# A two-layer hybrid block in one planned instruction stream: a low-rank rest product moved from 64 to 128 rows, and RWKV row sums as single fp32 products

## The chip, the core and the metric

The kernel runs on one core of a Trainium2 chip. The metric is device time in microseconds (us) of one execution. Before the change three executions took 1990.63, 1990.66 and 1992.5 us; the median is 1990.66 us. The engines are TensorE (PE, with its weight loads listed apart as PEld), VectorE (DVE), ScalarE (ACT), GpSimd (POOL) and SyncE (SP, which issues almost all transfers).

## The reference, cut to what matters

Two layers work on a sequence of 1024 tokens and 1024 channels. Each layer normalises its input with an adaptive scale and shift, projects it onto 4680 columns, runs three branches on parts of the result (chunked latent attention, a chunked state-space scan, and an RWKV-7 recurrence), and adds the gated output projection back. The change touches the RWKV branch:

```python
w_lo = token_shift(w_lo, mu_w)
a_lo = token_shift(a_lo, mu_a)
w = jnp.exp(-DECAY_SCALE * jax.nn.sigmoid((w0 + jnp.tanh(w_lo) @ w_lora_b).astype(f32)))
a = jax.nn.sigmoid((a0 + a_lo @ a_lora_b).astype(f32))
kk = k * heads(k_k)
kk = kk / jnp.maximum(jnp.sqrt(jnp.sum(kk * kk, axis=-1, keepdims=True)), 1e-12)
y = wkv7_scan(r, w, k, v, -kk, kk * a)
y = y + jnp.sum(r * k * r_k.astype(f32), axis=-1, keepdims=True) * v
```

There are 8 heads of 64 channels. `w_lo` and `a_lo` have 64 channels each, so the two low-rank products contract over 64 values. The two sums over a head's 64 channels (of the squared key, and of `r * k * r_k`) are the row sums of this document.

## The kernel before, in words

Channels lie on the 128 partitions and tokens on the free axis. The sequence is cut into two halves of 512 tokens, so that with two layers there are four stages. A stage first does its dense work: 8 tiles of normalised input, each split into a high part in fp32r and the rest (`a`, `b` in `make_h`, 16 tiles of the pool `h2`), and 37 column tiles of the input projection. Each column tile takes 24 products of 128x128 weights with 512 tokens: high weight with high input, high with rest, rest with high, for 8 contraction tiles. In the trace these are the rows `ps<-h,wh` and `ps<-h,wl`, since the tiles of `h2` are called `h`. ACT copies a finished tile out of PSUM (`ct<-ps`), and a transfer puts it into memory (`U<-ct`). For stages 2 and 3 the dense work begins with the output projection of layer 0, whose inputs are split into pairs of `h2` tiles by `y_split`.

The branches read `U` back. RWKV works on a pair of heads at a time, four pairs in a stage, so the function `rwkv_a1` and its follower `rwkv_a2` run 16 times. For each pair:

- two low-rank products. A product in fp32r keeps only part of the mantissa, so the input is split. `wa[0]` holds the high part of the 64 decay channels twice, once for each half of the partitions; the weight tile `lora` holds the high part of the 64 weight rows in one half of the partitions and their rest in the other. The first product over 128 rows therefore adds high x high and high x rest. A second product over 64 rows adds the input's rest (`wa[2]`) times the high weights. The same is done for the other 64 channels. These rows read `ps<-wa,lora`; the 64-row ones are `64*128 64x512`.
- the row sum `pq` (line 788 of the kernel before): the squared key is split by ACT into `leafh` and by DVE into `leafl`, and two fp32r products with two columns of a block-of-ones matrix (`bones_r`) give 2 rows of 512 sums.
- the row sum `pbn` (line 834): the same with all 128 columns of `bones_r`, which spreads each head's sum over its 64 partitions.

The row sum `pq` is copied to SBUF, goes through memory and scales a triangular inverse (`tinv_a`, the long chain of small DVE operations on `Q`, `rq` and `tmp`). `pbn` is multiplied by `v` and stored as `sp` for the end of the branch.

Beside this runs preparation for the next stage: loads of the modulation matrix land in `ct` tiles and DVE adds them up into `ac` (`ada_acc`); when a sum is complete, PE transposes it (`ps<-cst,ac`, in `colsum`) and DVE writes 4 columns of scale or shift (`md`).

Nothing is issued as it is written. Every operation is recorded, and a planner (`Plan.order`) then lists all of them in the order of a modelled time: each has a cost from a table, a rank, dependencies, and waits for a free buffer of its pool. RWKV has a higher rank than the other branches, and both have a higher rank than the `ac` sums. Each engine then executes its own list strictly in order. The planner's table charges extra for a product whose contraction needs another row mode than the one before it (`DRAIN`), and charges an fp32 product with at most 64 weight columns one short price whatever its length. These are the planner's assumptions, not measurements. A change of one operation therefore moves all lists. All recorded operations have one line in the trace (L396), so the rows are told apart by their tiles.

Of the kernel before, what the change touches and what calls it, by code (L numbers as in the profile page):

```python
# [10 lines left out]
F32R = mybir.dt.float32r  # L11
I32 = mybir.dt.int32
AF = mybir.ActivationFunctionType
# [4 lines left out]
P = 128  # L18
KT = 8
HT = 512  # L20
# [23 lines left out]
C_ID, C_MD, C_SM, C_BO, C_IF, C_SG, C_S4, C_M1 = 0, 128, 256, 768, 896, 897, 898, 902  # L44
NCST = 1030

N_H2, N_RT, N_RI, N_RQ, N_RL, N_CT, N_WR, N_WL, N_WH, N_B2 = 18, 5, 2, 2, 3, 4, 3, 3, 3, 17
N_BK, N_GG, N_BX, N_AR, N_BM, N_TT, N_RV, N_GT = 1, 2, 3, 1, 1, 2, 2, 2
RW_T = 0
N_EZ = 1  # L50
# [21 lines left out]
SG0 = "bbgggggg"  # L72
SBP, SBC, SCH = "ra", "ra", 2
SRB = "tf"
PQ = 1
PB = 1
PX = "b2"
WAT = "rv"
LOT = "rl"
# [318 lines left out]
def hybrid_layers_kernel(ctx: ExitStack, tc: tile.TileContext, A, out):  # L398
    nc = tc.nc
    plan = Plan(tc)  # L400
    V, S, G, PE, SP = (plan.engine(e, q) for e, q in ((nc.vector, "V"), (nc.scalar, "S"), (nc.gpsimd, "G"),
                                                      (nc.tensor, "P"), (nc.sync, "Q")))
    TQ, AL, AS, BL, BM, BS, EQ = SP, S, S, S, SP, S, SP

    cpool = ctx.enter_context(tc.tile_pool(name="cpool", bufs=1))
    lpool = ctx.enter_context(tc.tile_pool(name="lpool", bufs=1))
# [16 lines left out]
    def nm(s):  # L423
        ctr[0] += 1
        return f"{s}{ctr[0]}"
# [26 lines left out]
    def s1(n, tag=None, bufs=None):  # L452
        if bufs:
            return sm.tile([P, n], F32, name=nm("s"), tag=tag or f"s{n}", bufs=bufs)
        return sm.tile([P, n], F32, name=nm("s"), tag=tag or f"s{n}")

    def bank(tag):
        return ps.tile([P, HT], F32, name=nm("ps"), tag=tag, bufs=PSB[tag])

    def mm(o, lhsT, rhs, start=True, stop=True):  # L460
        PE.matmul(o, lhsT, rhs, start=start, stop=stop)

    def f32(ap):
        return ap.bitcast(F32)
# [7 lines left out]
    def hs_(e):  # L472
        return slice(64 * e, 64 * e + 64)
# [7 lines left out]
    bones = cst[:, C_BO:C_BO + 128]  # L481
# [3 lines left out]
    Ez = [cpool.tile([P, 2, 4, 128], F32, name=f"Ez{i}") for i in range(N_EZ)]  # L485
    for z in Tz + Ez:
        G.memset(z, 0.0)
    turn = [0]
    nhalf = cpool.tile([P, 8], F32, name="nhalf")
    V.memset(nhalf, -0.5)  # L490

# [7 lines left out]
    for e in range(2):  # L499
        SP.dma_start(cst[64:128, C_MD + 64 * e:C_MD + 64 * e + 64], A["cst"][64:128, C_MD + 64 * (1 - e):C_MD + 64 * (1 - e) + 64])  # L500
    SP.dma_start(mD1[64:128], A["cst"][64:128, C_MD:C_MD + 128])
    bones_r = cpool.tile([P, 128], F32R, name="bones_r")
    S.activation(bones_r, bones, AF.Copy)
    cth = s1(8)
    S.activation(cth, craw, AF.Tanh, scale=0.5)
    V.scalar_tensor_tensor(cth, cth, 1.0, craw, op0=ALU.add, op1=ALU.mult)
# [228 lines left out]
    def shifted(src, d, muc, omc, alloc):  # L735
        raw, o = ri(), alloc()
        AL.dma_start(raw, src)
        S.activation(o, raw[:, 3:HT + 3], AF.Identity, scale=d["om"][:, omc:omc + 1])
        V.scalar_tensor_tensor(o, raw[:, 2:HT + 2], d["pp"][:, muc:muc + 1], o, op0=ALU.mult, op1=ALU.add)
        return o  # L740

    def rwkv_in(d, U):
        wa = shifted(U[T_WA], d, PP_MUWA, 12, WATS[WAT])
        S.activation(wa[0:64], wa[0:64], AF.Tanh)
        WW, AA, lo = (lpool.tile([P, HT], F32R, name=nm("wa"), tag=f"wa{i}") for i in range(3))
        for e, o in ((0, WW), (1, AA)):
            for i in range(2):
                S.activation(o[hs_(i)], wa[hs_(e)], AF.Copy)
            V.tensor_tensor(lo[hs_(e)], wa[hs_(e)], f32(o[hs_(e)]), op=ALU.subtract)
        return WW, AA, lo  # L750

    def c8(ap):
        return ap.rearrange("p (c t) -> p c t", c=8)

    def rwkv_a1(d, U, p, wa):
        pp = d["pp"]
        r = shifted(U[T_R + p], d, PP_MUR + p, p, rt)
        k = shifted(U[T_K + p], d, PP_MUK + p, 4 + p, rt)
        v = shifted(U[T_V + p], d, PP_MUV + p, 8 + p, rv)
        fs = slice(128 * p, 128 * p + 128)  # L760
        pw = bank("ra")
        mm(pw, d["lora"][0][:, fs], wa[0], stop=False)
        mm(pw, d["lora"][0][0:64, fs], wa[2][0:64], start=False)
        lw = rt()
        S.activation(lw, pw, AF.Tanh, scale=0.5, bias=d["w0a0h"][:, p:p + 1])
        pa = bank("ra")
        mm(pa, d["lora"][1][:, fs], wa[1], stop=False)
        mm(pa, d["lora"][1][64:128, fs], wa[2][64:128], start=False)
        th = rt()
        S.activation(th, pa, AF.Tanh, scale=0.5, bias=d["w0a0h"][:, 4 + p:5 + p])  # L770
        V.tensor_scalar(lw, lw, -0.5 * DECAY, -0.5 * DECAY, op0=ALU.mult, op1=ALU.add)
        V.tensor_tensor_scan(lw, smask, lw, 0.0, op0=ALU.mult, op1=ALU.add)
        Pt = rt((P, 8, 65))
        V.memset(Pt[:, :, 0:1], 1.0)
        S.activation(Pt[:, :, 1:65], c8(lw), AF.Exp)
        iP = rt()
        S.activation(iP, lw, AF.Exp, scale=-1.0)
        sq = lw
        S.activation(sq, k, AF.Square, scale=pp[:, PP_KK + p:PP_KK + p + 1])
        m = rt()  # L780
        V.tensor_scalar(m, th, d["kah"][:, p:p + 1], d["omka"][:, p:p + 1], op0=ALU.mult, op1=ALU.add)
        V.tensor_scalar(th, th, d["kkh"][:, p:p + 1], d["kkh"][:, p:p + 1], op0=ALU.mult, op1=ALU.add)
        V.tensor_tensor(m, m, k, op=ALU.mult)
        V.tensor_tensor(th, th, k, op=ALU.mult)
        PC = s1(8, "PC", 4)
        for e in range(2):
            V.tensor_copy(PC[hs_(1 - e)], Pt[hs_(e), :, 64])
        pq = bank("ra")
        if PQ:
            hi, lo = WATS[PX](dt=F32R, leaf="leafh"), WATS[PX](dt=F32R, leaf="leafl")  # L790
            split(sq, hi, lo)
            mm(pq[0:2, :], bones_r[:, 0:128:64], hi, stop=False)
            mm(pq[0:2, :], bones_r[:, 0:128:64], lo, start=False)
        else:
            mm(pq[0:2, :], bones[:, 0:128:64], sq)
        S.activation(sq[0:2], pq[0:2], AF.Copy)
        qd = dr.tile([4, 8, 32], F32, name=nm("qd"), tag="qd")
        for e in range(2):
            qv = sq[e:e + 1].rearrange("o (c b t) -> o c b t", c=8, b=2)
            for b in range(2):  # L800
                AS.dma_start(qd[2 * e + b].unsqueeze(0), qv[:, :, b])
        return dict(r=r, k=k, v=v, th=th, m=m, Pt=Pt, iP=iP, PC=PC, qd=qd)

    def rwkv_a2(d, p, u):
# [29 lines left out]
        pbn = bank("ra")  # L834
        if PB:
            hi, lo = WATS[PX](dt=F32R, leaf="leafh"), WATS[PX](dt=F32R, leaf="leafl")
# [191 lines left out]
    def rwkv(l, d, U, hf, yd):  # L1028
        if hf == 0:
            lora_in(l, d)  # L1030
        wa = rwkv_in(d, U)
        us = [None] * 5

        def t_ab(p):
            tinv_a(us[p])
            tinv_b(us[p])
        us[0] = rwkv_a1(d, U, 0, wa)
        rwkv_a2(d, 0, us[0])
        t_ab(0)
# [176 lines left out]
    def split(src_ap, hi, lo, scale=1.0, eng=None):  # L1216
        S.activation(hi, src_ap, AF.Copy, scale=scale)
        if scale == 1.0:
            (eng or V).tensor_tensor(lo, src_ap, f32(hi), op=ALU.subtract)
        else:  # L1220
            V.scalar_tensor_tensor(lo, src_ap, scale, f32(hi), op0=ALU.mult, op1=ALU.subtract)
# [532 lines left out]
```

## Time and profile before

| what | value |
|---|---|
| median of three executions | 1990.66 us |
| profiled execution, whole | 1993.3 us |
| its span, first to last instruction | 1991.4 us |
| mean granted TensorE clock | 0.972 |
| PE busy | 1848.3 us, 93% |
| DVE busy | 1615.6 us, 81% |
| ACT busy | 1211.8 us, 61% |
| transfers | 341.31 MB, queue of SP 58.5% of 16 engines' span |

A row of the timeline gives the start, the busy time of the merged instructions, engine, operation, the tiles written and read, shapes and count; in brackets the idle time ahead and what ended it. The matmul ends are modelled: a product of 512 columns is shown as 0.39 us long although the next starts 0.23 us later. What a product costs in a stream is therefore read from start to start. An fp32 product is recorded as two instructions, a transpose or an fp32r product as one.

### The profile page before, as it was taken

The numbers are of one execution on the slowest core, as the hardware profiler recorded it, in microseconds if no ns is written. First come the engines' busy times: TensorE is split into PE (matmuls) and PEld (weight loads), VectorE is DVE, ScalarE is ACT, GpSimd is POOL, SyncE is SP. The second block draws the span as 40 slices with busy tenths as digits, with TensorE's granted clock in tenths as the row PEclk, the third lists the DMA queues.
The fourth block names the chain that finished last, engine by engine and source line by source line (L and its number), as shares of the span: only waits on it lengthen the run. The fifth ranks groups of instructions, "written<-read, shape, count | busy, mean of one in ns | idle before, by whom it ended". The sixth has DMA issues, their size and how long they took to land. (4 is left out here: it accounts for less than half of the span.)

```text
span 1991.4 us, 32320 instructions
## 1 busy us (share of the span) xinstructions
PE 1848.3 (93%) x10220; PEld 1450.4 (73%) x10220; DVE 1615.6 (81%) x4002; ACT 1211.8 (61%) x2520; POOL 202.9 (10%) x302
## 2 busy tenths in 40 slices
PE   5899978999999996999999999999999999999997
PEld 3677756777777774777787777787777877777775
DVE  7798886888987898887678887878787888778766
ACT  6555565666555665746656647666656657676653
POOL 2100010001010101011100010002011010000101
PEclk9999988999999997999999999999999999999998
DMA  7676655755666576753555475855457556663542
GB/s 243 212 192 172 184 169 151 216 159 171 182 155 178 162 218 185 239 160 119 159 141 161 136 209 164 253 157 159 119 150 169 146 172 183 204 200 104 167 145 93
DMA packets 273371, 341.31 MB, mean 171 GB/s; under 512 B 79153, under 2 KB 132017, under 8 KB 273201
## 3 DMA queue, kind: packets, MB, share of 16 engines
q1 hardware_dynamic: 273200, 339.25, 58.5%
q8 instruction: 81, 1.33, 0.3%
q14 instruction: 90, 0.73, 0.1%
HBM read 254.67 MB, written 84.47 MB: 170 GB/s over the span
## 5 line engine op out<-in xcount | busy, mean ns | idle before, releaser
L396 PE MATMUL ps<-h,wh 128*128 128x512 f32 x3136 | 1021.1, 409 | 41.7 <-ACT ct L396 23.3
L396 PEld LDWEIGHTS ps<-h,wh 128*128 128x128 f32 x3136 | 580.8, 191 | 179.9 <-ACT ct L396 36.1
L396 PE MATMUL ps<-h,wl 128*128 128x512 f32 x1568 | 590.2, 408 | 2.3 <-DVE wl L396 2.3
L396 PE MATMUL ps<-b,b 128*128 128x128 f32 (+4 forms) x1512 | 388.9, 359 | 11.8 <-ACT b L396 4.0
L396 ACT ACTIVATE wh<-wr 128x512 fp32r<-128x512 f32 (+1 forms) x398 | 245.6, 620 | 220.1 <-PE ps L396 178.4
L396 PEld LDWEIGHTS ps<-h,wl 128*128 128x128 f32 x1568 | 296.8, 191 | 61.5 <-issue 4.8
L396 DVE TENSOR_TENSOR wl<-wr,wh 128x512 fp32r<-128x512 f32 (+1 forms) x398 | 268.7, 680 | 81.6 <-ACT wh L396 64.0
L396 PEld LDWEIGHTS ps<-b,b 128*128 128x128 f32 (+1 forms) x1512 | 232.2, 183 | 75.5 <-ACT b L396 18.1
L396 ACT ACTIVATE b<-b 128x512 f32<-128x512 f32 (+3 forms) x222 | 137.3, 626 | 71.6 <-DVE b L396 24.8
L396 DVE TENSOR_TENSOR b<-b,b 128x512 fp32r<-128x512 f32 (+4 forms) x178 | 121.4, 688 | 33.1 <-ACT b L396 32.2
L396 ACT ACTIVATE b<-ps 128x512 f32<-128x512 f32 (+3 forms) x201 | 99.5, 509 | 68.2 <-PE ps L396 63.0
L396 DVE TENSOR_TENSOR tmp<-Q,rq 128x60 f32<-128x60 f32 (+24 forms) x496 | 106.6, 215 | 5.7
L396 DVE TENSOR_TENSOR rq<-rq,tmp 128x60 f32<-128x60 f32 (+24 forms) x496 | 105.6, 213 | 5.2
L396 PEld LDWEIGHTS ps<-bx,gg 128*128 128x128 f32 x512 | 77.6, 194 | 41.3 <-ACT bx L396 14.4
L396 ACT ACTIVATE ct<-ps 128x512 f32<-128x512 f32 x150 | 88.1, 590 | 29.5 <-DMA U<-ct 9.9
L396 PE MATMUL ps<-cst,b 128*128 128x128 f32 x452 | 81.6, 282 | 15.2 <-POOL b L396 14.8
L396 POOL COPY halo<-ct 128x3 f32<-128x3 f32 x84 | 32.7, 389 | 616.2 <-ACT ct L396 616.1
L396 PE MATMUL ps<-bx,gg 128*128 128x64 f32 x512 | 83.5, 273 | 12.6 <-ACT bx L396 7.1
L396 ACT ACTIVATE b<-ps,s,s 128x512 f32<-128x512 f32 (+2 forms) x96 | 64.1, 669 | 39.3 <-DVE s L396 33.6
L396 PEld LDWEIGHTS ps<-cst,b 128*128 128x128 f32 x452 | 58.8, 146 | 30.9 <-POOL b L396 14.8
L396 DVE SCALAR_TENSOR_TENSOR h<-ps,md,h 128x512 f32<-128x512 f32 x72 | 53.7, 748 | 26.6 <-PE ps L396 26.1
L396 PEld LDWEIGHTS ps<-gg,bk 128*128 128x128 f32 x512 | 65.0, 193 | 14.1 <-issue 5.9
(196 smaller groups left out, 2598.7 us busy)
## 6 DMA issues: line engine op xcount, KB each, us to landing
wr<-in_w_in_dram SPq DMA_DIRECT2D x282, 256.0 KB
U<-ct SPq DMA_DIRECT2D x84, 257.5 KB
wr<-in_w_out_dram SPq DMA_DIRECT2D x80, 256.0 KB
U<-ct SPq DMA_DIRECT2D x64, 256.0 KB
ct<-in_ada_dram SPq DMA_DIRECT2D x64, 256.0 KB
ri<-U SPq DMA_DIRECT2D x52, 257.5 KB
b<-accd SPq DMA_DIRECT2D x96, 128.0 KB
ct<-yd SPq DMA_DIRECT2D x48, 256.0 KB
```

The lines of the kernel that those rows point to most:

```text
L396: o.fn(*o.args, **o.kw)
```

## The change

The input's rest is no longer one tile of which a half is used for each product. Two permanent tiles `Lz[0]` and `Lz[1]` of 128 rows are set to zero once in the half that is not used, and each stage writes its rest into the other half. The second low-rank product runs over all 128 rows; the rows of the weight tile's rest meet zeros. The two flags `PQ` and `PB` go to 0: each row sum is one fp32 product of the unsplit tile with the fp32 `bones`, and the copies into `leafh`, the subtractions into `leafl` and the tile `bones_r` go. The pool `h2` has 17 tiles in place of 18.

```diff
-N_H2, ... = 18, ...
+N_H2, ... = 17, ...
-PQ = 1
-PB = 1
+PQ = 0
+PB = 0
...
+    Lz = [cpool.tile([P, HT], F32R, name=f"Lz{i}") for i in range(2)]
+    for i, z in enumerate(Lz):
+        S.activation(z[64 - 64 * i:128 - 64 * i], Ez[0][64 - 64 * i:128 - 64 * i, i].rearrange("p c t -> p (c t)"), AF.Copy)
...
-    bones_r = cpool.tile([P, 128], F32R, name="bones_r")
-    S.activation(bones_r, bones, AF.Copy)
...
-        WW, AA, lo = (lpool.tile([P, HT], F32R, name=nm("wa"), tag=f"wa{i}") for i in range(3))
-        for e, o in ((0, WW), (1, AA)):
+        WW, AA = (lpool.tile([P, HT], F32R, name=nm("wa"), tag=f"wa{i}") for i in range(2))
+        for e, o, lo in ((0, WW, Lz[0]), (1, AA, Lz[1])):
...
-        mm(pw, d["lora"][0][0:64, fs], wa[2][0:64], start=False)
+        mm(pw, d["lora"][0][:, fs], Lz[0], start=False)
...
-        mm(pa, d["lora"][1][64:128, fs], wa[2][64:128], start=False)
+        mm(pa, d["lora"][1][:, fs], Lz[1], start=False)
```

The code that the flags choose between was there before:

```python
pq = bank("ra")
if PQ:
    hi, lo = WATS[PX](dt=F32R, leaf="leafh"), WATS[PX](dt=F32R, leaf="leafl")
    split(sq, hi, lo)
    mm(pq[0:2, :], bones_r[:, 0:128:64], hi, stop=False)
    mm(pq[0:2, :], bones_r[:, 0:128:64], lo, start=False)
else:
    mm(pq[0:2, :], bones[:, 0:128:64], sq)
```

The planner lists the program anew. On PE its rows (equal neighbours merged) go from 6791 to 6769, on DVE from 3905 to 3878, on ACT from 2148 to 2110. Two places follow. The first is PE where stage 0 reaches the `pq` row sum of its third head pair (about row 870 before, row 820 after); `h` with `wh` and `wl` is the dense work, and the transposes `cst,gg` and `cst,bk` are the RWKV steps behind the row sum. Before:

```order
L396 MATMUL ps_517<-h_260,wh_522 128x512
L396 MATMUL ps_517<-h_261,wh_522 128x512
L396 MATMUL ps_517<-h_260,wl_523 128x512
L396 MATMUL ps_724<-leafh_725,bones_r 2x512
L396 MATMUL ps_724<-leafl_726,bones_r 2x512
L396 MATMUL ps_730<-cst,gg_672 128x128 x4
L396 MATMUL ps_731<-cst,gg_672 128x128 x4
L396 MATMUL ps_732<-cst,bk_671 128x128 x4
L396 MATMUL ps_733<-cst,bk_671 128x128 x4
```

After:

```order
L396 MATMUL ps_498<-h_261,wh_503 128x512
L396 MATMUL ps_716<-rt_709,cst 2x512
L396 MATMUL ps_498<-h_262,wh_503 128x512
L396 MATMUL ps_498<-h_261,wl_504 128x512
L396 MATMUL ps_720<-cst,gg_666 128x128 x4
L396 MATMUL ps_953<-cst,b_950 128x128 x4
L396 MATMUL ps_721<-cst,gg_666 128x128 x4
L396 MATMUL ps_959<-cst,b_957 128x128 x4
L396 MATMUL ps_722<-cst,bk_665 128x128 x4
L396 MATMUL ps_723<-cst,bk_665 128x128 x4
L396 MATMUL ps_508<-h_170,wh_510 128x512
L396 MATMUL ps_508<-h_171,wh_510 128x512
```

The one product now stands two dense products ahead of the column tile's end, two column tiles earlier in the dense work, and a whole dense tile follows the transposes.

The second place is PE at the end of stage 1's dense work, where the transposes of the `ac` sum for the next layer's shift stand. Before:

```order
L396 MATMUL ps_1626<-h_1262,wh_1631 128x512
L396 MATMUL ps_1626<-h_1261,wl_1632 128x512
L396 MATMUL ps_2029<-cst,s_2027 128x128 x4
L396 MATMUL ps_1635<-cst,ac_1547 128x128 x4
L396 MATMUL ps_2049<-b_2014,b_2047 128x512
L396 MATMUL ps_2049<-b_2016,b_2047 128x512
L396 MATMUL ps_2049<-b_2014,b_2048 128x512
```

After:

```order
L396 MATMUL ps_1610<-h_1237,wl_1613 128x512
L396 MATMUL ps_1619<-cst,ac_1531 128x128
L396 MATMUL ps_1610<-h_1239,wh_1615 128x512
L396 MATMUL ps_1619<-cst,ac_1531 128x128
L396 MATMUL ps_1610<-h_1240,wh_1615 128x512
L396 MATMUL ps_1619<-cst,ac_1531 128x128
L396 MATMUL ps_1610<-h_1239,wl_1616 128x512
L396 MATMUL ps_2034<-b_1981,b_2030 128x512
L396 MATMUL ps_1610<-h_1241,wh_1615 128x512
```

The transposes stood behind the stage's last dense product and now stand in the middle of its last column tile, with the second half of that tile, 12 products, behind the first of them.

More of the change, by code (lines that the diff above doesn't have):

```diff
@@ L45 @@
 NCST = 1030
-N_H2, N_RT, N_RI, N_RQ, N_RL, N_CT, N_WR, N_WL, N_WH, N_B2 = 18, 5, 2, 2, 3, 4, 3, 3, 3, 17
+N_H2, N_RT, N_RI, N_RQ, N_RL, N_CT, N_WR, N_WL, N_WH, N_B2 = 17, 5, 2, 2, 3, 4, 3, 3, 3, 17
 N_BK, N_GG, N_BX, N_AR, N_BM, N_TT, N_RV, N_GT = 1, 2, 3, 1, 1, 2, 2, 2
@@ L749, in rwkv_in @@
             V.tensor_tensor(lo[hs_(e)], wa[hs_(e)], f32(o[hs_(e)]), op=ALU.subtract)
-        return WW, AA, lo
+        return WW, AA
     def c8(ap):
```

## The prediction, made before the changed kernel ran

> **What bounds the kernel now.** I read first the page's busy times, then the busy time by stages, then PE's timeline at the operations that change, and last the waits of PE. The page:
>
> ```profile
> span 1991.4 us, 32320 instructions
> PE 1848.3 (93%) x10220; PEld 1450.4 (73%) x10220; DVE 1615.6 (81%) x4002; ACT 1211.8 (61%) x2520; POOL 202.9 (10%) x302
> ```
>
> PE is busy for 93% of the span, so its work sets the time in the main. But the share is a mean. The windows (length, then busy us and count of PE, PEld, DVE, ACT, POOL, then the granted clock, transfers' share and GB/s) show two regimes:
>
> ```profile
> 0.00:790.00 790.00, 694.89 (x3766) 533.22 (x3767) 664.32 (x1691) 473.89 (x984) 87.69 (x142) 0.95 0.63 184
> 790.00:1970.00 1180.00, 1146.22 (x6426) 912.12 (x6425) 940.21 (x2296) 732.71 (x1528) 108.98 (x155) 0.99 0.56 164
> 282.00:316.00 34.00, 15.54 (x55) 10.37 (x54) 28.72 (x82) 17.59 (x34) 4.94 (x6) 0.63 0.27 83
> 757.00:800.00 43.00, 27.25 (x105) 19.39 (x105) 37.06 (x85) 24.59 (x44) 6.24 (x7) 0.76 0.64 197
> ```
>
> From 790 us on PE is 97% busy and nothing else matters much. Before that it stands still for 95 of 790 us, and in the two worst places, 282 to 316 and 757 to 800 us, DVE is busy for 28.7 of 34 and 37.1 of 43 us while PE waits. So a microsecond of PE work counts everywhere, and a microsecond of DVE or ACT work counts in part of the first 790 us. Both bad places also show a low granted clock, 0.63 and 0.76: 0.37 x 34 = 12.6 us and 0.24 x 43 = 10.3 us of full clock are gone there on top of the waits.
>
> **The rest pass (PE).** PE's timeline at the first head pair (start, length, tiles, shape, count):
>
> ```profile
> 94.55 0.63 PE L396 MATMUL ps<-h,wh 128*128 128x512 f32 x2
> 95.02 0.39 PE L396 MATMUL ps<-h,wl 128*128 128x512 f32 x1
> 95.24 0.41 PE L396 MATMUL ps<-wa,lora 128*128 128x512 f32 x1
> 95.49 0.40 PE L396 MATMUL ps<-h,wh 128*128 128x512 f32 x1
> 95.82 0.49 PE L396 MATMUL ps<-wa,lora 64*128 64x512 f32 x1
> 96.24 0.50 PE L396 MATMUL ps<-h,wl 128*128 128x512 f32 x1
> 96.58 0.63 PE L396 MATMUL ps<-h,wh 128*128 128x512 f32 x2
> ...
> 99.32 0.40 PE L396 MATMUL ps<-h,wl 128*128 128x512 f32 x1
> 99.64 0.50 PE L396 MATMUL ps<-wa,lora 64*128 64x512 f32 x1
> 100.08 0.66 PE L396 MATMUL ps<-cst,b 128*128 128x128 f32 x4
> 100.49 0.47 PE L396 MATMUL ps<-h,wh 128*128 128x512 f32 x1
> ```
>
> Two 128-row products take 94.55 to 95.02, so 0.23 us each. From 95.49 to 96.58 there are three products, the middle one over 64 rows, and they take 1.09 us instead of 0.69: 0.40 us for the step into 64 rows and out of it. Where four transposes follow (0.35 us for four, 1532.55 to 1532.90 below), 99.32 to 100.49 is 1.17 us for 0.23 + 0.23 + 0.35 = 0.81 us of work: 0.36 us. A 128-row product in that place costs 0.23 us like its neighbours. There are 32 such passes:
>
> ```profile
> L396 PE MATMUL ps<-wa,lora 64*128 64x512 f32 x32 | 16.1, 504 | 0.0
> L396 PE MATMUL ps<-leafl,bones_r 128*128 128x512 f32 x16 | 7.3, 459 | 0.0
> L396 PE MATMUL ps<-leafl,bones_r 128*2 128x512 f32 x16 | 7.0, 437 | 1.1 <-DVE leafl L396 1.1
> L396 PE MATMUL ps<-leafh,bones_r 128*2 128x512 f32 x16 | 6.3, 396 | 3.1 <-ACT leafh L396 3.1
> ```
>
> So 32 x 0.38 = **-12.2 us** of PE time (11.5 to 12.8).
>
> **The row sums (PE).** Two fp32r products of 0.23 us become one fp32 product, 32 times. The trace of before has no fp32 product of 512 columns; the nearest are those with 256 columns, two records each. Here are two of them, four records:
>
> ```profile
> 1531.45 0.39 PE L396 MATMUL ps<-h,wh 128*128 128x512 f32 x1
> 1531.69 1.02 PE L396 MATMUL ps<-b,b 128*128 128x256 f32 x4
> 1532.55 0.60 PE L396 MATMUL ps<-cst,gg 128*128 128x128 f32 x4
> 1532.90 0.47 PE L396 MATMUL ps<-h,wh 128*128 128x512 f32 x1
> ```
>
> 1531.69 to 1532.55 is 0.86 us for 512 columns. So a row sum costs 0.86 instead of 0.46, or 32 x 0.40 = **+12.8 us**. At the top, four times the fp32r price of 0.23 is 0.92: +14.7 us. At the bottom, the 16 sums with two weight columns could cost half, since only a small part of the array is used: 16 x (0.43 - 0.46) + 16 x 0.40 = +5.9 us. I take the full price for them, because the fp32r product with two weight columns gains nothing by it:
>
> ```profile
> 110.79 0.39 PE L396 MATMUL ps<-leafh,bones_r 128*2 128x512 f32 x1
> 111.03 0.62 PE L396 MATMUL ps<-h,wl 128*128 128x512 f32 x2
> ```
>
> The next one starts 0.24 us later, as behind 128 columns. The Trainium skill (TensorE: Matmul & The Clock Gate, section Back-to-back issue gap) has the time in a stream depend on the moving columns alone, which would also give the full price. PE's balance is **+0.6 us**, from -6.9 to +3.2.
>
> **The splits (ACT and DVE).** What goes, by shape:
>
> ```profile
> L396 ACT ACTIVATE leafh<-rt 128x512 fp32r<-128x512 f32 x32 | 20.0, 624 | 4.0 <-DVE rt L396 3.0 <-PE ps L396 0.8
> L396 DVE TENSOR_TENSOR leafl<-rt,leafh 128x512 fp32r<-128x512 f32 x32 | 21.9, 685 | 4.8 <-ACT leafh L396 4.5
> L396 DVE TENSOR_TENSOR leafl<-rt,leafh 128x512 fp32r<-128x512 f32 x15 | 10.3, 687 | 0.5 <-ACT leafh L396 0.4
> ```
>
> ACT loses 20.0 us and DVE 21.9 us; the last row, of the window up to 790 us, says that 15 of the 32, 10.3 us on DVE, fall into the first regime. Behind 790 us PE's own queue hides them: worth nothing. Before it I let half reach the end, **-5.2 us** (0 to -10.3), since in that stretch DVE is busy 84% of the time and PE idle 12%. Against more than half speaks that each engine also waits on the others and on transfers there.
>
> PE also waited for the splits themselves: 3.1 and 1.1 us in the rows above. Nearly all of it is one place:
>
> ```profile
> 282.87 0.39 PE L396 MATMUL ps<-h,wl 128*128 128x512 f32 x1
> 286.32 0.39 PE L396 MATMUL ps<-leafh,bones_r 128*2 128x512 f32 x1 [3.06 <-ACT leafh L396]
> 287.44 0.59 PE L396 MATMUL ps<-leafl,bones_r 128*2 128x512 f32 x1 [0.74 <-DVE leafl L396]
> ```
>
> Now the sum reads the square directly, and in the new order it stands inside a dense tile two tiles earlier, with 24 dense products behind the transposes that follow. I count **-3 us** (0 to -4.2). What is late next there is the chain of transposes and ACT copies behind the sum, which one dense tile of 5.5 us (24 x 0.23) covers in part. The granted clock of 0.63 follows this wait in the same window; if the wait goes, some of the 12.6 us may too. The Trainium skill (the same page, section What's actually happening) says that an idle window of about 3.4 us halves the clock until a busy one has passed. The trace agrees with that here (a stop of 3.45 us from start to start, then the low clock). By the rule, a gain or a loss of one such stop counts up to twice. I leave it out of the sum and put it into the range.
>
> **One h tile fewer.** During dense work 16 tiles of `h2` are in use and two are spare: room for one split pair ahead of time. With one spare the pair's second tile waits for the first freed one. The price of a late pair is its split:
>
> ```profile
> L396 ACT ACTIVATE h<-ct x4: 629/630/633, 773.1 to 781.6; 128x512 fp32r<-128x512 f32 x4
> L396 DVE TENSOR_TENSOR h<-ct,h x4: 693/693/693, 773.8 to 782.2; 128x512 fp32r<-128x512 f32 x4
> ```
>
> That is 0.63 + 0.69 = 1.3 us. Five phases start with loads or splits into this pool (stages 1 to 3 and the two last output projections), so 0 to 6.6 us; other branches' products fill most of these places, so I take one of the five, **+1.3 us**. Setting up `Lz` adds two ACT copies at the start, where ACT waits for transfers: nothing, and 1.2 us without that cover.
>
> **The sum.** +0.6 - 5.2 - 3 + 1.3 = -6.3 us against the profiled execution's own 1993.3 us (span 1991.4 us): 1987.0 us. That execution lies 2.6 us above the median of 1990.66, so the forecast is **1984 us**, a change of -0.3%.
>
> **The rivals.** *PE alone counts:* DVE and ACT relief is hidden everywhere. For it speaks the 97% after 790 us, against it the two windows. Then only +0.6 + 1.3 remain: 1993 us, within 0.2%, which is about what a measurement of this kernel can tell from no change (4 us).
>
> *A new wait in the new order, slower.* The whole list is planned anew on assumed costs, and PE runs its list in order. The place is the `ac` sum at the end of stage 1:
>
> ```profile
> 755.63 0.40 PE L396 MATMUL ps<-h,wl 128*128 128x512 f32 x1
> 756.92 0.65 PE L396 MATMUL ps<-cst,s 128*128 128x128 f32 x4 [0.89 <-POOL s L396]
> 766.71 1.11 PE L396 MATMUL ps<-cst,ac 128*128 128x128 f32 x4 [9.14 <-DVE ac L396]
> L396 DVE SCALAR_TENSOR_TENSOR ac<-ct,cact,ac x3: 740/745/747, 763.4 to 765.9; 128x512 f32<-128x512 f32 x3
> ```
>
> PE waited 9.14 us for DVE, with all dense products done. In the new order 12 dense products stand behind these transposes. If DVE comes as late again, they wait with PE, and so do the h tiles that they would free and the four split pairs of the next output projection: 12 x 0.23 + 4 x 1.3 = 8.0 us later than now, and the low clock of 10.3 us may come a second time. I price it at 16 us: 1984 + 16 = 2000 us. For it speaks that DVE's list has this work at the lowest rank and DVE is full there; against it, that DVE has less to do by then. It decides once DVE is later than PE by more than the 12 products' 2.8 us.
>
> *Both reliefs in full:* the sums with two columns cost half (-6.9), all of DVE's 10.3 and PE's 4.2 us are gained: 1990.66 - 21.4 = 1969 us. *The rest pass gains nothing* (the zero rows cost the same step): 1984 + 12.2 = 1996 us; every 128-row product in the rows above runs at 0.23 us, so this is unlikely.
>
> **How the numbers follow.** Forecast 0.45, of which 0.38 lies below -0.2% and 0.07 within; PE alone 0.20 (0.02 faster, 0.13 same, 0.05 slower); new wait 0.23, slower; both reliefs 0.08, faster; rest pass without gain 0.04, slower. Together: faster 0.48, same 0.20, slower 0.32. The forecast's own range is 1977 to 1991 us. The range for 8 in 10 reaches from just below the two full reliefs to a little beyond the new wait: 1967 to 2004 us.
>
> **What would show it.** Right: three consecutive products around a rest pass 0.69 us apart; an fp32 row sum of 0.86 us from start to start with 128 and with two weight columns; DVE at about 1594 and ACT at about 1192 us busy; PE's idle time lower before 790 us and unchanged behind it. Wrong: a row sum with two columns that costs 0.43 us, PE waiting for DVE at `ac` or elsewhere for longer than 9.14 us, more windows with a clock below 0.8, or waits of PE for `h` at the starts of the stages.

## The result, and the profile after

The changed kernel is **slower by 0.56%**: 2000.82 us median of 8 executions (1996.5 to 2011.22) against 1990.8 us for the kernel before beside it (8 executions, 1988.2 to 1992.5), a ratio of 1.0056 with a 95% interval of 1.004 to 1.0072 (this and all later ratios are estimated from all executions of a session; the two medians alone would give 1.0050). In a second session it was 1.0050 (1.0034 to 1.0066). The forecast was 1984 us. The profiled execution took 2007.91 us, 7 us above the median, so differences of single rows count for less than the ratio.

The page of the changed kernel, the two lines that were shown of before:

```profile
span 2006.1 us, 32214 instructions
PE 1860.4 (93%) x10220; PEld 1458.9 (73%) x10220; DVE 1598.6 (80%) x3970; ACT 1201.6 (60%) x2491; POOL 199.5 (10%) x302
```

DVE is 17.0 us and ACT 10.2 us less busy; the splits that are gone had 21.9 and 20.0 us. On ACT a part of the relief is used up: the new list has seven loads of activation tables instead of five (2.6 us more), and the two copies that set up `Lz` take 1.2 us. PE is 12.1 us more busy, where a balance of +0.6 was forecast. The windows of the changed kernel (columns as in the prediction):

```profile
0.00:790.00 790.00, 699.73 (x3757) 541.13 (x3757) 653.12 (x1671) 466.87 (x967) 85.23 (x141) 0.95 0.63 181
790.00:1970.00 1180.00, 1138.84 (x6370) 901.24 (x6371) 924.08 (x2269) 724.26 (x1508) 106.76 (x156) 0.99 0.56 165
282.00:316.00 34.00, 22.62 (x98) 16.01 (x97) 29.24 (x83) 16.98 (x32) 5.85 (x6) 0.87 0.39 118
757.00:800.00 43.00, 37.23 (x159) 27.68 (x160) 33.42 (x91) 22.53 (x41) 4.69 (x7) 0.98 0.78 245
100.00:282.00 182.00, 159.80 (x839) 123.64 (x838) 152.60 (x368) 100.18 (x204) 13.52 (x27) 0.92 0.62 171
594.00:757.00 163.00, 149.33 (x865) 117.63 (x865) 133.57 (x314) 96.37 (x198) 12.05 (x18) 0.91 0.60 169
```

In the two bad stretches of before things are better now: PE is busy 22.62 instead of 15.54 us in the first and 37.23 instead of 27.25 us in the second, and the granted clock rises from 0.63 to 0.87 and from 0.76 to 0.98. But the stretches ahead of them, which were good before, are bad now. The same two windows of the kernel before:

```profile
594.00:757.00 163.00, 153.81 (x931) 118.96 (x930) 140.02 (x336) 100.77 (x211) 14.41 (x20) 0.98 0.66 185
100.00:282.00 182.00, 170.88 (x910) 132.49 (x910) 159.01 (x381) 105.94 (x215) 14.33 (x28) 0.96 0.66 185
```

There PE loses 11.1 us of work from 100 to 282 us and 4.5 us from 594 to 757 us, and the clock falls from 0.96 to 0.92 and from 0.98 to 0.91. The waits moved; they did not go: PE stands still for 145.7 us of the whole span, where it was 143.1 us. The worst new one, in PE's timeline of the changed kernel (start, length, tiles, shape, count, and in brackets the idle time and what ended it):

```profile
206.59 0.62 PE L396 MATMUL ps<-h,wh 128*128 128x512 f32 x2
207.04 0.39 PE L396 MATMUL ps<-h,wl 128*128 128x512 f32 x1
213.90 1.09 PE L396 MATMUL ps<-cst,b 128*128 128x128 f32 x4 [6.47 <-DVE b L396]
...
219.10 0.63 PE L396 MATMUL ps<-h,wl 128*128 128x512 f32 x1
219.52 1.48 PE L396 MATMUL ps<-h,wh 128*128 128x512 f32 x3
220.80 0.63 PE L396 MATMUL ps<-h,wl 128*128 128x512 f32 x1
...
222.20 0.63 PE L396 MATMUL ps<-h,wh 128*128 128x512 f32 x2
222.67 0.39 PE L396 MATMUL ps<-h,wl 128*128 128x512 f32 x1
```

PE's list has transposes of `b` there, a tile of another branch that DVE makes, and DVE is full (7.00 of the 7 us in the windows below). PE waits 6.47 us, with the dense work behind it in its list. After the wait four products take 219.10 to 220.80, 0.43 us each, and only from about 222 us again 0.23 us. The windows of that place in the changed kernel show the granted clock at 0.51 for it:

```profile
207.00:214.00 7.00, 0.53 (x3) 0.14 (x3) 7.00 (x21) 3.56 (x9) 0.00 (x0) 0.83 0.39 117
214.00:222.00 8.00, 7.04 (x21) 5.47 (x22) 5.29 (x9) 6.30 (x18) 0.34 (x1) 0.51 0.65 174
222.00:232.00 10.00, 10.00 (x57) 7.11 (x56) 6.92 (x13) 1.89 (x4) 0.00 (x0) 1.00 0.33 76
```

So a wait costs more than its length: 6.5 us standing, then 8 us at half clock, of which about 4 are lost. Since a product at half clock counts as busy for longer, this also explains a small part of PE's higher busy time: by the clock record of the traces PE is busy at half clock for 78.1 us in the changed kernel and for 72.3 us in the kernel before, which is some 3 of the 12.1 us.

What PE waited for in the first 850 us (total us, times, longest), a choice of rows. The changed kernel, then the kernel before:

```profile
PE ps L396 <- DVE b L396: 20.2, 7, 6.5
PE ps L396 <- ACT h L396: 11.9, 10, 2.4
PE ps L396 <- DVE gg L396: 7.2, 4, 2.5
```

```profile
PE ps L396 <- ACT h L396: 10.6, 10, 1.9
PE ps L396 <- DVE ac L396: 9.1, 1, 9.1
PE ps L396 <- DVE b L396: 3.4, 4, 1.4
PE ps L396 <- ACT leafh L396: 3.1, 1, 3.1
PE ps L396 <- DVE gg L396: 2.8, 3, 2.2
```

The waits for `ac` and `leafh`, 12.2 us, are gone, and those for `b` and `gg` are up by 21.2 us. All waits of PE together hardly change (96.1 us before, 98.6 us now). What is left to do behind 850 us tells how far each kernel had come. Before, then after:

```profile
850.00:2010.00 1160.00, 1094.35 (x6075) 870.52 (x6073) 899.53 (x2196) 692.79 (x1439) 111.48 (x156) 0.98 0.54 157
```

```profile
850.00:2010.00 1160.00, 1109.06 (x6173) 878.99 (x6172) 906.36 (x2231) 697.13 (x1451) 112.35 (x158) 0.98 0.54 158
```

At 850 us the changed kernel has 1109.06 us of PE time ahead of it instead of 1094.35 us, 14.7 us more, and its span is 14.7 us longer. In these two executions the whole difference is there by 850 us, that is in the first two stages and the change to the third. It is mostly PE's busy time (12.1 us) and little its idle time (2.6 us); besides the 3 us of half clock, the operations that changed are some 3.5 us dearer by the rows further down, and the rest of the busy time isn't explained by any run.

### The profile page after: what moved, and what is told of

Same layout as the page of the kernel before. It is cut to its first block, busy times and chain, and to the rows that moved or that the text cites. A ratio compares the mean times of both kernels' runs of the same rounds, so it can differ in the third digit from the quotient of the medians.

```text
span 2006.1 us, 32214 instructions
## 1 busy us (share of the span) xinstructions
PE 1860.4 (93%) x10220; PEld 1458.9 (73%) x10220; DVE 1598.6 (80%) x3970; ACT 1201.6 (60%) x2491; POOL 199.5 (10%) x302
## 5 line engine op out<-in xcount | busy, mean ns | idle before, releaser
L396 PE MATMUL ps<-b,b 128*128 128x512 f32 (+4 forms) x1512 | 379.1, 354 | 15.0 <-DVE b L396 7.9
L396 ACT ACTIVATE ct<-ps 128x512 f32<-128x512 f32 x150 | 88.2, 590 | 29.6 <-PE ps L396 12.3
L396 PEld LDWEIGHTS ps<-bx,gg 128*128 128x128 f32 x512 | 78.1, 195 | 37.3 <-DVE bx L396 10.8
L396 PE MATMUL ps<-gg,bk 128*128 128x128 f32 x512 | 73.9, 288 | 6.2 <-DVE gg L396 4.8
```

What stands on the lines that cost most here:

```text
L396: o.fn(*o.args, **o.kw)
```

## The experiments

Theories: **D**, the changed operations cost more than the prediction had it. **H**, the missing h tile. **O**, the order that the planner makes anew. Later, inside O: **T**, the piece of the list around the change from stage 1 to stage 2; **S**, the loss is spread over the list; **M**, the planner's price for the row sum with two columns (the front part tells of it) is far too short and leads it astray; **R**, the rest pass with 17 tiles leads it astray. All kernels compute the whole reference. Ratios are to the kernel before in the same session, with 95% intervals; its medians there were 1994.8, 1996.0, 1991.8, 1996.6 and 1991.0 us, so only ratios compare across groups.

### Operations or order

For three kernels the planner is shown the old operations and makes its list from them; when the list is issued, the new operations are put in place of the old ones. In `dir17` all operations of the change stand in exactly the order of `h17`; in `dirrs18` only the row sums are new, in the order of the kernel before; `dirlz17` (last group) has the rest pass alone. The edit, in short (`alt` is what is issued in an operation's place; `single` is a row sum, `rest` the rest pass):

```diff
+    def single(src, hi, lo, o, w_r, w):
+        n = len(plan.ops)
+        split(src, hi, lo)
+        mm(o, w_r, hi, stop=False)
+        for x in plan.ops[n:]:
+            x.alt = ()
+        mm(o, w_r, lo, start=False).alt = ((nc.tensor.matmul, (o, w, src), dict(start=True, stop=True)),)
+    def rest(o, w, x, h):
+        mm(o, w[h], x[h], start=False).alt = ((nc.tensor.matmul, (o, w, x), dict(start=False, stop=True)),)
```

`h17` is the kernel before with one h tile fewer, planned anew:

```diff
-N_H2, ... = 18, ...
+N_H2, ... = 17, ...
```

> The kernel before with 17 h tiles in place of 18 and nothing else; the planner lists everything anew. Theory H (the missing tile costs the time: late split pairs at the starts of the stages): 1999 us or more, +8 to +10, with waits for h at the starts of stages 2 and 3. Theory O (any new order of this program may gain or lose this much, the operations are innocent): anywhere from 1980 to 2010, not tied to h. Theory D (the changed operations cost it): about 1992, since none of them is changed.

Measured: 1993.8 us, **0.9999** (0.9981 to 1.0016). H falls: in this list the tile costs nothing that shows.

> The changed operations put into the order of the 17-tile kernel before: the planner sees the old operations and makes the same list as for the run with 17 h tiles alone; at the place of each pair of row-sum products the one fp32 product is issued, the splits are left out, and the rest pass runs over 128 zero-padded rows. Against that run: theory D +8 to +10 us; theory O 0 to -9 us (my sum for the operations: +0.6 on PE, up to -8 from the splits that are gone), whatever the two kernels' distance to the kernel before.

Measured: 1994.05 us, **0.9995** (0.9977 to 1.0013). All the changed operations together, in the old order, cost nothing that shows: D falls.

> Only the row sums as single fp32 products, in the unchanged order of the kernel before with 18 h tiles; splits left out. PE has 32 x 0.40 = 12.8 us more work. If PE bounds everywhere: 2003 us. If the splits' 20 us on ACT and 22 us on DVE count in half of the first 790 us: 1995. Theory O: it does not reach the changed kernel's loss by itself for any other reason than PE's 12.8 us.

Measured: 1996.71 us, **1.0009** (0.9991 to 1.0028). PE is 10.7 us more busy than before (1859.0 against 1848.3), the time rises by 1.8 us (-1.8 to +5.6):

```profile
span 2000.0 us, 32241 instructions
PE 1859.0 (93%) x10220; PEld 1447.6 (72%) x10220; DVE 1599.3 (80%) x3970; ACT 1193.7 (60%) x2488; POOL 199.9 (10%) x302
```

`rs18` has the same operations, but the planner sees them and makes a new list:

```diff
-PQ = 1
-PB = 1
+PQ = 0
+PB = 0
```

> The same row sums with the order planned anew, 18 h tiles, rest pass over 64 rows as before. Theory D: the same time as with the old order, within 3 us. Theory O: it differs from the run with the old order by more than 5 us, in either direction.

Measured: 1984.39 us, **0.9945** (0.9918 to 0.9972). Between `dirrs18` and `rs18` no operation differs, only the order, and the time differs by 0.64%. So an order can cost or bring as much as the whole verdict is large. PE waits for `b` 9.0 us in its first 850 us, against 20.2 us in the changed kernel:

```profile
PE ps L396 <- DVE b L396: 9.0, 5, 4.4
```

### Which piece of the list, and the planner's price

`after2` is the changed kernel again. `xyx` issues the changed kernel's list with the list of `dir17` in the middle (between dense products 1536 and 1960, the change from stage 1 to stage 2); `yxy` the other way round.

> The changed kernel once more, as the reference of this set. If its loss belongs to the program and not to one chip or one set of runs: again +0.4 to +0.7% against the kernel before. If its loss was a matter of that set: within 0.2%.

Measured: 2006.49 us, **1.0050** (1.0034 to 1.0066).

> The changed operations throughout. Order: the 17-tile list of the run dir17 up to dense product 1536 of 4704 (about 665 us), the changed kernel's list up to product 1960 (about 890 us), the 17-tile list for the rest. Theory T (the changed kernel loses in the order of the change from stage 1 to stage 2, where its profile falls behind by 12 us of equal PE work): +0.3 to +0.6% against the kernel before, near the changed kernel. Theory S (the loss is spread, every stretch of the order adds a little): +0.1%.

> The reverse: the changed kernel's list, but with the 17-tile list between dense products 1536 and 1960. Theory T: within 0.2% of the kernel before, as the run dir17 was. Theory S: +0.4 to +0.5%, close to the changed kernel.

Measured: `yxy` 2021.19 us, **1.0124** (1.0101 to 1.0148); `xyx` 2014.17 us, **1.0088** (1.0065 to 1.0111). Both are slower than either list alone: I put this down to the two seams, since each list had prepared other work for what comes behind them, but no run shows it. The totals say nothing on T or S.

`aftm2` is the changed kernel with the planner's price for the two-column row sum put right (the short price, 0.10 us, then holds for at most 128 streamed columns, and this sum is charged 0.89 us; the trace shows 0.95 us for it, not the 0.86 us of the expectation below):

```diff
-        return ("D", 103) if m <= 64 else ("F", 1.73 * max(m, k) + 2)
+        return ("D", 103) if m <= 64 and k <= 128 else ("F", 1.73 * max(m, k) + 2)
```

> The changed kernel with one planner cost put right: an fp32 product with two weight columns and 512 columns is planned at the price of one with 128 weight columns (the trace shows 0.86 us for both) instead of 103 ns; the operations are the same, the lists are new. Theory M (the mispriced row sum misleads the planner and is why the new order is bad): faster than the changed kernel by 6 us or more, at or below the kernel before. Theory O (any new order lands anywhere): 1980 to 2010, with no tie to the price.

Measured: 1991.05 us, **0.9978** (0.9962 to 0.9995). The very same operations as the changed kernel, and the loss is gone. This looked like M; the next two groups ask whether it is.

### How much does any other list differ?

One assumed latency is moved by one nanosecond, which changes nothing that the planner means, but sets off another list: of the 8408 places in PE's list, 6762 hold another operation in `befn` than in the kernel before. `befn`, `aftn` and `aftm2n` are the kernel before, the changed kernel and `aftm2` with it; `rs18m2` is `rs18` with the price put right.

```diff
-            "PS": 197, ...
+            "PS": 198, ...
```

> The changed kernel, planned with one latency of the planner's table raised from 197 to 198 (PE to ACT); nothing else. The operations are the changed kernel's. Theory O (a new list lands anywhere): off the changed kernel's +0.5% by 4 us or more with about even odds. Theory M (the mispriced row sum is the cause): stays at +0.3 to +0.7% of the kernel before.

Measured: 2002.91 us, **1.0048** (1.0035 to 1.0062).

> The changed kernel with the row sum's price put right and the same nudge of 1. Theory M: stays below the kernel before, -0.1 to -0.5%. Theory O: may land anywhere from -0.5 to +0.7%.

Measured: 1981.4 us against 1991.8 us, **0.9945** (0.9932 to 0.9957). With `rs18` this is the fastest list found, and faster than both kernels; it computes the same.

> The kernel before with the same nudge of 1. Theory O: a shift of several us in either direction from a list that means the same. Theory M says nothing of it; if the planning is robust, within 0.1%.

Measured: 1989.64 us, **0.9988** (0.9976 to 0.9999).

> The row sums alone (rest pass over 64 rows, 18 h tiles), planned with the right price of the two-column sum. Its mispriced form ran at -0.55%. Theory M: faster still, -0.6 to -1.0%. Theory O: anywhere, so most likely slower than that good draw.

Measured: 1983.09 us, **0.9950** (0.9933 to 0.9967). With the wrong price `rs18` was as fast (0.9945), so the wrong price alone need do no harm; and `aftm2` and `aftm2n`, of one meaning, differ by 0.33%.

The profile of `aftm2n`, which executes the operations of the changed kernel: page, PE's wait for `b` up to 850 us, and the windows from 850 us and at the place of the 6.47 us wait:

```profile
span 1976.9 us, 32259 instructions
PE 1843.5 (93%) x10220; PEld 1445.9 (73%) x10220; DVE 1595.0 (81%) x3970; ACT 1191.5 (60%) x2489; POOL 193.2 (10%) x302
```

```profile
PE ps L396 <- DVE b L396: 6.2, 4, 4.0
```

```profile
850.00:2010.00 1160.00, 1085.82 (x6002) 860.47 (x6000) 876.24 (x2157) 670.13 (x1396) 103.75 (x153) 0.99 0.54 156
197.00:222.00 25.00, 24.62 (x168) 19.68 (x167) 20.51 (x39) 17.34 (x40) 0.42 (x1) 1.00 0.74 213
```

PE is busy 16.9 us less than in the changed kernel with the same 10220 matmuls (1843.5 against 1860.4), and idle 12.3 us less (133.4 against 145.7). The wait for `b` at 207 us doesn't exist: in 197 to 222 us PE is busy for 24.62 of 25 us at full clock, where it was 17.57 us in the changed kernel.

### The rest pass without the wrong price, and a third draw

`lz17` is the other half of the change alone: the rest pass on 128 rows and 17 tiles, with the split row sums of before, planned anew.

```diff
-PQ = 0
-PB = 0
+PQ = 1
+PB = 1
...
+    bones_r = cpool.tile([P, 128], F32R, name="bones_r")
+    S.activation(bones_r, bones, AF.Copy)
```

The planner knows what the rest pass on 64 rows costs: by `DRAIN` it charges the 64-row product and the 128-row one behind it 0.195 us more each, 0.39 us in all, and measured are 0.36 to 0.40 us. So no operation of `lz17` is priced far off. `lz17n` is `lz17` with 197 put to 198. `aftv` and `aftm2v` are the changed kernel and `aftm2` with another nudge:

```diff
-EXTRA = {"S": 70, "V": 93, ...
+EXTRA = {"S": 70, "V": 94, ...
```

> The other part of the change alone: the rest pass on 128 rows with 17 h tiles; the row sums stay split products. The planner plans it anew, and no row sum is priced wrongly in it. M (the wrong price of the two-column row sum led the order astray): not slower than before, and by the price of the operations (32 products of 0.36 to 0.40 us less) up to 0.6% faster, about 1980 to 1990. O as a lottery (any new order may come out badly, whatever its prices): anything from 1980 to 2005, without a link to the price. R (the pair of rest pass and one h tile fewer leads the planner astray by itself): about 2000, as the changed kernel.

Measured: 2004.81 us, **1.0041** (1.0019 to 1.0064).

> lz17 with one assumed latency moved by one nanosecond, so that the order is another one of the same meaning. M: within 0.4% of lz17 and not slower than before. Lottery: may differ from lz17 by as much as the changed kernel differs from before (0.5%), in either direction. R: about 2000 again.

Measured: 2013.27 us, **1.0084** (1.0056 to 1.0113), the slowest whole list, with no wrong price in it. M falls as the cause: the wrong price is neither needed for the loss (`lz17`, `lz17n`) nor enough for it (`rs18`). Both runs came out as R had it, but R alone doesn't hold either: `aftm2`, `aftm2n` and the later `aftm2v` have the rest pass and 17 tiles too and lose nothing.

> The changed kernel with another assumed cost moved by one nanosecond (a wait's extra cost on VectorE, 93 to 94): a third order with the wrong price. M: +0.3 to +0.6% against before (about 2000), with a wait of several microseconds for VectorE near 207 us and a loss at the change of the stages. Lottery: could come out at 0 or below as well.

Measured: 2000.96 us, **1.0013** (0.9995 to 1.0032).

> The changed kernel with the row sum's price put right, and the same nudge (93 to 94): a third order with the right price. M: -0.1 to -0.6% against before (about 1980 to 1990), without the wait near 207 us. Lottery: could come out at +0.5% as well.

Measured: 1997.47 us, **1.0001** (0.9979 to 1.0023). Without and with the right price the three pairs of lists differ by 0.72, 1.03 and 0.12%, each within one session, each time in favour of the right price; but lists of one meaning differ among themselves by up to 0.56% (`aftm2n` and `aftm2v`), so three pairs don't settle what the price is worth.

### The rest pass in the old order, and a third list of the row sums

> The rest pass on 128 rows with 17 h tiles, issued in exactly the order that the planner made for the kernel before with 17 h tiles; the row sums stay split products. O (the order planned anew is what costs): not slower than before. The price of the operations alone, 32 products of 0.36 to 0.40 us less, would give about 12 us or -0.6% if TensorE sets the time all through; the runs with both parts and with the row sums alone in that same order (0.9995 and 1.0009) leave about -0.1% for it, so if the order holds the gain back, -0.1 to -0.2%. The rest pass bad in itself (for the permanent tiles are written in place, and the next layer must wait for the last reader): +0.4% as lz17.

Measured: 1987.88 us, **0.9988** (0.9971 to 1.0005). The rest pass is not bad in itself. It is also not worth what PE saves. The pages of `h17` and of `dirlz17`, which run in the same order, and the group of the second low-rank product in each (busy us, mean ns):

```profile
span 1992.2 us, 32331 instructions
PE 1850.0 (93%) x10220; PEld 1449.0 (73%) x10220; DVE 1613.1 (81%) x4002; ACT 1208.4 (61%) x2520; POOL 200.2 (10%) x302
L396 PE MATMUL ps<-wa,lora 64*128 64x512 f32 x32 | 16.5, 514 | 0.0
```

```profile
span 1987.3 us, 32333 instructions
PE 1839.8 (93%) x10220; PEld 1447.0 (73%) x10220; DVE 1613.6 (81%) x4002; ACT 1208.6 (61%) x2522; POOL 198.1 (10%) x302
L402 PE MATMUL ps<-Lz,lora 128*128 128x512 f32 x32 | 13.7, 427 | 0.0
```

PE is 10.2 us less busy; its idle time, span less busy, grows from 142.2 to 147.5 us. In this pair of executions half of the gain turns into waits, and the ratio gives -0.12%, 2.4 us (from 5.8 less to 1.0 more).

> The row sums as single products alone, 18 h tiles, planned anew with one assumed latency moved by one nanosecond: another order of the same meaning, the wrong price in it. O as a lottery: anything from -0.6 to +0.6% against before. R (only with the rest pass and 17 tiles does the planner go astray): -0.4 to -0.6%, as the two orders of it so far.

Measured: 1988.5 us, **0.9985** (0.9974 to 0.9996), against 0.9945 and 0.9950 for the other two lists of the row sums alone.

### All lists side by side

Each matmul is priced by the median distance from start to start of its shape. A column gives the time at which the matmuls begun so far add up to 175, 350, 500, 675 or 1675 us of such PE work, as a difference to the kernel before. It comes from one profiled execution of each kernel, which may lie some microseconds off its median. The last columns are the PE busy time left at 850 us and the ratio on record. Work that a kernel adds or saves on PE is left out of the differences as far as the medians have it, so they show waits and clock in the main.

```
kernel    sums    rest pass  list             175    350    500    675   1675   left   ratio
before    split   64 rows    old                0      0      0      0      0   1094   1
befn      split   64 rows    1 ns             -2.2   -7.4   -1.3   -2.4   -4.0   1091   0.9988
h17       split   64 rows    17 tiles         +1.0   -1.3   -1.9   -0.0   -1.2   1093   0.9999
dirrs18   single  64 rows    old              +0.5   -6.4   -8.1   -7.2   -5.4   1103   1.0009
dirlz17   split   128 rows   that of h17      -0.6   -3.1   -3.8   -3.1   +0.9   1085   0.9988
dir17     single  128 rows   that of h17       0.0   -7.9   -9.8  -10.4   -0.5   1098   0.9995
rs18      single  64 rows    new             +10.5  -23.0  -26.6  -13.0  -21.1   1091   0.9945
rs18n     single  64 rows    new, 1 ns        +5.7  -24.2  -27.4  -21.3  -14.4   1090   0.9985
rs18m2    single  64 rows    new, price       +7.1  -20.0  -15.3  -33.2  -18.7   1079   0.9950
after     single  128 rows   new             +16.8   +0.4   -0.6   +9.9   +8.2   1109   1.0056
aftn      single  128 rows   new, 1 ns       +15.4   -1.5   -2.8   +6.8   +3.1   1106   1.0048
aftv      single  128 rows   new, 1 ns       +13.8   +2.2   +0.4   +4.2   -0.3   1105   1.0013
aftm2     single  128 rows   new, price       +3.4   -1.9   -1.0  -10.8   -9.6   1090   0.9978
aftm2n    single  128 rows   new, price, 1 ns -0.5   -9.2   -8.4  -16.8  -22.1   1086   0.9945
aftm2v    single  128 rows   new, price, 1 ns +14.2 -18.8  -20.3  -16.5  -10.4   1087   1.0001
lz17      split   128 rows   new              +1.2  -12.2  -12.4  +14.9  +15.7   1101   1.0041
lz17n     split   128 rows   new, 1 ns        +1.5  -11.5  -19.3  +17.8  +24.6   1108   1.0084
```

In these executions two places make most of the difference, up to 350 us of work and 500 to 675 us, the change from stage 1 to stage 2; behind them the differences still move by up to 15 us, but in either direction, and single executions of one kernel differ by as much (the kernel before by 17.6 us within the first of these sessions). The new lists of the row sums keep 13 to 33 us there. The changed kernel's first list gains nothing at the first place and loses 10.5 us at the second (-0.6 to +9.9); the lists of `lz17` gain 12 to 19 us and lose 27 to 37.

**What is shown and what is open.** In an old order every part of the change, and the whole, lies between -0.12 and +0.09% (the intervals reach from -0.29 to +0.28%). In new lists these parts and the whole lie between -0.55 and +0.84%, and the changed kernel's own operations alone between -0.55 and +0.56%. So the order makes the verdict; the operations do not. Open is why all five lists with the rest pass and no put-right price came out slower (+0.13 to +0.84%), and all eight other newly planned lists at +0.01% or below. Lists of one meaning scatter by 0.1 to 0.6%, which is as wide as most of this difference; a cause beyond the draw (the price, the pools, the permanent tiles) is not shown. One row goes with the loss: PE's wait for DVE's `b` in the first 850 us is 15.4 to 20.2 us in the four slowest of these lists (the changed kernel, `aftn`, `lz17`, `lz17n`) and 3.0 to 11.1 us in the other nine. Whether it makes them slow or is only a sign of it, no run shows.

## Why the prediction was wrong

**The step that failed** is the sum's silence on the order. It took the new list's gains into the terms (the wait at 283 us, -3 us) and put its losses outside, into a rival with 0.23. The operations in the old order are worth -1.0 us (-4.6 to +2.6, `dir17`); the kernel as planned is worth +11 us (8.0 to 14.3, 0.56% of 1990.8). The 12 us between the two are the list. No term of the sum stands for it: the forecast took it that a list planned anew is as good as the one before.

**The slower rival** has the right sign and price, 2000 us, by another mechanism, so its price is luck. Its place, the `ac` sum at the end of stage 1, improved: PE's wait for `ac` is gone. The group of those transposes in the changed kernel:

```profile
L396 PE MATMUL ps<-cst,ac 128*128 128x128 f32 x36 | 9.8, 275 | 1.8 <-DVE rq L396 1.8
```

What came instead is waits for `b` and `gg`, at places that no term and no rival named. Rows of before could not name them: PE hardly waits for these tiles, 3.4 and 2.8 us in all. The 10.3 us of lost clock in that rival's price, like the 12.6 us of the other stretch, are also too many: PE was busy for only 27.25 of those 43 us and 15.54 of those 34 us, and a slow clock costs nothing while PE stands.

**The rest pass, -12.2 us:** right as PE time, wrong as time. Three products around a rest pass in the changed kernel:

```profile
95.86 0.39 PE L396 MATMUL ps<-h,wh 128*128 128x512 f32 x1
96.09 0.40 PE L396 MATMUL ps<-Lz,lora 128*128 128x512 f32 x1
96.33 0.40 PE L396 MATMUL ps<-h,wl 128*128 128x512 f32 x1
96.57 1.08 PE L396 MATMUL ps<-h,wh 128*128 128x512 f32 x4
```

95.86 to 96.57 is 0.71 us for three; 0.69 was forecast and 1.09 was the price before. PE's busy time falls by 10.2 us, the time by 2.4 us (`dirlz17`). "A microsecond of PE work counts everywhere" was the mistake: of the 10.2 us, 5.3 came back as waits in the traced pair. That an earlier PE meets the same late tiles would explain it, but isn't shown.

**The row sums, +12.8 us:** +10.7 us of PE busy time in the old order (`dirrs18`), and so +0.5 with the rest pass's -10.2, where +0.6 was forecast, but with both in one kernel PE's busy time was 6.4 us above that of `h17` (`dir17`, 1856.4 against 1850.0, in an execution 7 us above its median). The doubt on the sum with two weight columns goes the other way: it is not cheaper but dearer. Both forms in the changed kernel:

```profile
110.88 0.40 PE L396 MATMUL ps<-h,wl 128*128 128x512 f32 x1
111.20 1.02 PE L396 MATMUL ps<-rt,cst 128*2 128x512 f32 x2
112.16 0.96 PE L396 MATMUL ps<-h,wh 128*128 128x512 f32 x3
...
141.69 1.02 PE L396 MATMUL ps<-rt,cst 128*128 128x512 f32 x2
142.55 0.60 PE L396 MATMUL ps<-cst,b 128*128 128x128 f32 x4
```

That is 0.96 us with two columns and 0.86 with 128. All 16 sums with two columns take 0.95 us to the next start, and the product ahead of them takes 0.32 instead of 0.23 us; those with 128 take 0.86 to 0.96 us, but for one. By these rows 16 sums cost 0.58 us more each instead of 0.40, and the balance on PE is some +3.5 us (my estimate: 16 x 0.58 + 16 x 0.40 - 12.2). The rule of the moving columns that the prediction cites for the full price is given in that section of the Trainium skill (TensorE: Matmul & The Clock Gate, section Back-to-back issue gap) for a single product; for a stream the section lets the weight load count as well. The rows decide: the number of weight columns does matter here, though not as the doubt had it.

**The splits and PE's wait for them, -8.2 us together:** of the right size as far as it shows. The row sums in the old order cost 10.7 us of PE busy time and 1.8 us of time (-1.8 to +5.6), so the relief would be worth 8.9 us if each microsecond of PE counted in full, which the rest pass contradicts. In the table, which leaves most of PE's work out, `dirrs18` is 5.4 to 8.1 us ahead from 350 us of work on, in one execution.

**The h tile, +1.3 us:** -0.2 us (-3.8 to +3.2), and PE's waits for `h` up to 850 us hardly move (10.6 to 11.9 us).

**The sum in the old order** is -1.0 instead of -6.3 us. The miss of 5 us is the rest pass's, which brought 2.4 us instead of 12.2, partly made up by the row sums, which with their reliefs cost 1.8 us instead of 4.6 (12.8 less 8.2). Of what was to show the steps, the 0.71 us, the 0.86 us of the row sums with 128 columns and DVE at 1598.6 us (about 1594 expected) came; ACT at 1201.6 us (about 1192) did not; PE's idle time up to 790 us fell a little (95.1 to 90.3 us) but rose behind it (33.8 to 41.2 us). Of what was to show it wrong, "PE waiting for DVE at `ac` or elsewhere for longer than 9.14 us" came only in sum: no single wait for DVE is longer than 6.5 us, but those for `b` add up to 20.2 us. More stretches at a low clock did not come either: 13 at half clock with 108 us in all, where there were 12 with 110 us.

## What to carry to other kernels

Where a planner lists the whole program anew, a local edit is two changes: price the operations by issuing them in the old order, and price the list by drawing a few more lists of the same meaning; here the operations were worth 0.1% and the lists spread over more than 1%. A forecast for such a kernel should carry the spread of the lists as its main uncertainty, and a verdict of half a per cent on one list says little about the edit. PE time saved need not become time: here it was 2.4 of 10.2 us by the ratio, with an interval from 5.8 us gained to 1.0 us lost.

## What the runs showed of the hardware that was not expected

PE's busy time is no count of its work: the same 10220 matmuls of the same shapes were busy for 1860.4 us in one list and 1843.5 us in another. Products at half clock (0.43 us apart instead of 0.23 us) count for longer, and PE was busy at half clock for 78.1 us in the first and 49.0 us in the second, which makes some 14.5 of the 16.9 us. The Trainium skill (TensorE: Matmul & The Clock Gate, section What's actually happening) has the clock halve after an idle window; the 8 us at a clock of 0.51 behind the 6.47 us wait agree with it. A stop as long as the prediction's 3.45 us isn't needed: in the kernel before, a wait of 2.18 us that ended at 136.95 us was followed by 6.8 us at a clock of 0.50, and one of 1.88 us, ended at 927.91 us, by another 6.8 us. An fp32 product with 512 columns costs no less with two weight columns than with 128 (0.95 us against 0.86 us). And one kernel scatters more than one session shows: the kernel before ran at 1988.2 to 1992.5 us in the first session and at 1984.1 to 2004.4 us over the others.
